# The entry of a two-layer trunk's first layer: half of the input from ScalarE's queue, five buffers for scale and shift, and another order of sums and products

## The chip, the cores and the metric

One core of a Trainium2 chip runs the whole network as one program. The metric is the device time of one launch in microseconds (us). The median of three runs of the kernel before is 2196.83 us (2194.26 to 2197.61); one further execution, recorded by the hardware profiler, took 2200.38 us. All durations below come from that execution's trace.

## What is computed

Only the very start of the network is touched: the entry of layer 0, up to its first projection.

```python
c_act = jax.nn.silu(c)                                   # c: 1 x 1024
mod = c_act @ ada_w[0] + ada_b[0]                        # 1024 x 6144 weights
sh_m, sc_m, g_m, sh_f, sc_f, g_f = jnp.split(mod, 6, axis=-1)
h = rmsnorm(x, norm_g[0, 0]) * (1 + sc_m) + sh_m         # x: 1024 positions x 1024
bcx = h @ conv_in_w[0]                                   # 1024 x 3072
b_gate, c_gate, xh = jnp.split(bcx, 3, axis=-1)          # then a 3-tap causal conv, gates, conv_out_w
```

After it come layer 0's conv output and its squared-ReLU MLP, a shared key/value side, layer 1's latent attention, and layer 1's MLP. All tensors are 32-bit floats.

## The kernel before, in words

**Tiling.** D = 1024 is cut into KD = 8 blocks k of 128 features, the positions into NT = 8 tiles t of 128 rows (`xt[0..7]`, 128x1024, named y in the profile) and into two halves of 512 positions. TensorE multiplies 32-bit values as two parts: `split_w` (L162 to L164) makes a high part on ScalarE and a low part on VectorE, and `mm` (L158 to L160) does three matmuls of 128x512 for each product. `products(w, k, half, acc)` is one feature block times one half, into three PSUM banks (the groups b, c and x of 128 output columns): nine matmuls. The phase is passed twice, for the output columns m = 0 and m = 1; the first pass also makes the operands: 16 groups of nine for m = 0, then 16 for m = 1. The remaining columns are done in another way (`all_pairs`).

**What one block k needs in the first pass.** `ada(k)` loads the scale and shift columns of `ada_w[0]` for block k, 1 MB, into the tile `aw` (three buffers) by four transfers. `ada_end(k)` (L816 to L827) sums them over eight row blocks on VectorE into `av`, each times a column of silu(c): one TENSOR_SCALAR (L820) and seven SCALAR_TENSOR_TENSOR (L822); then TensorE adds over the partitions with two matmuls by a column of ones (L824, written as four fp32 passes in the trace), and VectorE makes scale and shift, `sh` (L825, L827). `turn(k, half)` transposes four x tiles on TensorE (L832); `scaled` (L835 to L839) applies `sh` twice on ScalarE, to the high part and to the full value, and VectorE subtracts for the low part. `weights(k, m)` loads 192 KB of `conv_in_w` and splits them. `norm_x(half)` (L895 to L897) makes each x row's root of the sum of squares on ScalarE (L245, L247) and divides on VectorE.

**Order.** TensorE's and SyncE's instructions stay in the order in which the code is written (`pinned`); VectorE's and ScalarE's are set by the tile scheduler. Each engine runs its list strictly in order. SyncE issues all loads of the phase; each takes one of eight completion semaphores in turn, so a load waits until the one eight places earlier has landed, whichever engine issued it. The first half runs LAG = 2 blocks ahead: `first_half(k+1)`, then `products(k, 0)`, then `second_half(k-1)` and `products(k-2, 1)`. The small vectors (gains, biases, taps: eight transfers into the tile `raw`) are issued from ScalarE's queue (L136 to L139), x from SyncE's (`load_x`).

## Time and profile before

| | |
|---|---|
| median of three runs | 2196.83 us (2194.26 to 2197.61) |
| profiled execution | 2200.38 us, of which the recorded span is 2198.6 us |
| first product matmul (128x512) begins | 26.15 us after the span's start |
| last product of the first pass (m = 0) ends, the first of m = 1 begins | 87.08 us |
| m = 1 | 87.08 to 119.06 us |
| TensorE busy, whole span | 2105.9 us (96%) |

From 121.9 us on TensorE works almost without a pause; the first 87 us are where it stands still. In the rows of the profile a name ending in q (SPq, ACTq) is the engine's queue of issued transfers, PEld is TensorE's weight load, PEclk the granted share of TensorE's full clock, "x6" the number of instructions merged into a row, and the part in brackets is how long the engine stood idle just before, and what ended that.

### The profile page before, as it was taken

The page shows a single profiled execution, that of the slowest core. Times are in us where ns is not written, and L with a number is a line of the kernel's source. Part 1 is how long each engine was busy: PE and PEld are TensorE (multiplying, and loading weights), DVE is VectorE, ACT ScalarE, POOL GpSimd, SP SyncE. Part 2 cuts the span into 40 slices and gives each one's busy share as a digit, 9 for nine tenths or more (in the row PEclk, how much of TensorE's full clock was granted, in tenths as well). Part 3 has the DMA queues.
Part 4 walks back from the last instruction along what each step waited for, and adds up shares of the span by engine and source line. Part 5 has one row for each costly group of instructions (what it writes and reads, how often), then busy time and mean ns, then how long its engine had stood idle before and what let it go on. Part 6 is the DMA issues. An engine that isn't in the chain of part 4 may idle for free.

```text
span 2198.6 us, 25300 instructions
## 1 busy us (share of the span) xinstructions
PE 2105.9 (96%) x9702; PEld 1730.7 (79%) x9702; DVE 1523.0 (69%) x2001; ACT 1053.3 (48%) x1501; POOL 4.0 (0%) x8
## 2 busy tenths in 40 slices
PE   4999999899999999999899999999899999999998
PEld 3778878678888788888777788878688887888886
DVE  6767766866665579766788776665865665566665
ACT  4533354745454444343665555564744444444422
POOL 0000000000000000000000000000000000000000
PEclk9999999999999999999999999999999999999999
DMA  7444464246543986454214231043244553852343
GB/s 222 127 126 143 126 209 145 77 153 191 168 158 114 327 277 209 157 171 146 82 52 128 76 103 53 25 153 130 77 154 159 184 174 139 304 180 96 121 138 115
DMA packets 233551, 323.61 MB, mean 147 GB/s; under 512 B 18165, under 2 KB 141394, under 8 KB 233430
## 3 DMA queue, kind: packets, MB, share of 16 engines
q1 hardware_dynamic: 198424, 244.11, 35.5%
q10 hardware_dynamic: 35006, 77.89, 9.3%
q8 instruction: 76, 1.25, 0.2%
q14 instruction: 45, 0.37, 0.1%
HBM read 244.35 MB, written 77.59 MB: 146 GB/s over the span
## 4 chain that ended last, share of the span: by engine, by line
PE 75%; DVE 13%; ACT 6%; DMA 4%; issue 2%; ACTq 0%; SPq 0%; DVEq 0%
PE one L160 38%; PE mm L160 18%; PE big L160 9%; PE tp L160 6%; DMA raw<-in_ada_w_dram 3%; ACT junk L245 2%; PE big L1281 2%; DVE y L302 2%; DVE raw L303 2%; DVE acc L185 1%; PE tp L1307 1%; DVE y L296 1%; DVE small L1284 1%; ACT small L247 1%; PE tp L398 1%
## 5 line engine op out<-in xcount | busy, mean ns | idle before, releaser
L160 PE MATMUL one<-slot,uphi 128*128 128x512 f32 x1224 | 378.9, 391 | 0.0
L160 PE MATMUL big<-slot 128*128 128x512 f32 x1536 | 353.5, 390 | 0.9 <-DVE slot L164 0.4
L160 PEld LDWEIGHTS big<-slot 128*128 128x128 f32 x1536 | 287.6, 188 | 61.0 <-ACT y L745 1.1
L160 PEld LDWEIGHTS one<-slot,uphi 128*128 128x128 f32 x1224 | 231.3, 189 | 48.5 <-issue 0.5
L160 PE MATMUL one<-slot,uplo 128*128 128x512 f32 x612 | 241.3, 394 | 8.1 <-ACT y L564 2.3
L164 DVE TENSOR_TENSOR uplo<-raw,uphi 128x1024 fp32r<-128x1024 f32 x127 | 153.0, 1220 | 138.0 <-ACT uphi L163 137.9
L160 PE MATMUL one<-ring,ring 128*128 128x512 f32 x864 | 199.9, 392 | 5.5 <-DVE ring L164 5.5
L163 ACT ACTIVATE ring<-w 128x1024 fp32r<-128x1024 f32 x84 | 88.9, 1059 | 229.5 <-PE tp L160 121.0
L160 PEld LDWEIGHTS one<-ring,ring 128*128 128x128 f32 x864 | 162.8, 189 | 41.6 <-DVE ring L164 4.7
L163 ACT ACTIVATE uphi<-raw 128x1024 fp32r<-128x1024 f32 x127 | 134.5, 1060 | 121.1 <-PE one L160 89.4
L160 PE MATMUL mm<-slot,uphi 128*128 128x512 f32 x520 | 165.9, 400 | 9.5 <-DVE slot L363 9.3
L164 DVE TENSOR_TENSOR ring<-w,ring 128x1024 fp32r<-128x1024 f32 x84 | 102.6, 1221 | 82.5 <-ACT ring L163 82.4
L185 DVE SCALAR_TENSOR_TENSOR acc<-raw,csil,acc 128x1024 f32<-128x1024 f32 x88 | 112.7, 1281 | 44.8 <-DMA raw<-in_ada_w_dram 42.1
L160 PEld LDWEIGHTS one<-slot,uplo 128*128 128x128 f32 x612 | 115.6, 189 | 35.6 <-ACT y L489 3.3
L160 PE MATMUL mm<-ring,ring 128*128 128x512 f32 x576 | 139.6, 391 | 0.0
L160 PE MATMUL tp<-ring,ring 128*128 128x512 f32 x576 | 138.7, 389 | 0.0
L160 PEld LDWEIGHTS mm<-ring,ring 128*128 128x128 f32 x576 | 107.6, 188 | 23.5 <-issue 0.7
L160 PEld LDWEIGHTS tp<-ring,ring 128*128 128x128 f32 x576 | 108.1, 188 | 22.5
L160 PEld LDWEIGHTS mm<-slot,uphi 128*128 128x128 f32 x520 | 98.8, 192 | 32.6 <-DVE slot L363 10.8
L489 ACT ACTIVATE y<-one 128x512 f32<-128x512 f32 x66 | 39.0, 590 | 164.0 <-PE one L160 115.5
L160 PE MATMUL one<-slot,s 128*128 128x512 f32 x468 | 112.5, 389 | 0.6 <-DVE s L164 0.6
L160 PE MATMUL mm<-slot,uplo 128*128 128x512 f32 x260 | 106.3, 409 | 4.3 <-ACT slot L360 2.3
(255 smaller groups left out, 3513.0 us busy)
## 6 DMA issues: line engine op xcount, KB each, us to landing
ha<-y ACTq DMA_DIRECT2D x168, 256.0 KB, 4.3
raw<-ha SPq DMA_DIRECT2D x84, 512.0 KB, 4.1
raw<-in_ada_w_dram SPq DMA_DIRECT2D x80, 512.0 KB, 3.9
raw<-in_mlp_up_w_dram SPq DMA_DIRECT2D x70, 512.0 KB, 4.5
w<-in_mlp_down_w_dram SPq DMA_DIRECT2D x48, 512.0 KB, 6.0
raw<-hd SPq DMA_DIRECT2D x32, 512.0 KB, 4.3
hd<-y ACTq DMA_DIRECT2D x24, 512.0 KB, 2.9
xs<-raw ACTq DMA_DIRECT2D x24, 512.0 KB, 3.1
```

The costliest lines, as they stand in the source:

```text
L160: nc.tensor.matmul(out_, lhs[a], rhs[b], start=first and i == 0, stop=last and i == 2, skip_group_check=more)
L163: nc.scalar.activation(hi, src, AF.Copy)
L164: nc.vector.tensor_tensor(lo, src, hi.bitcast(F32), op=ALU.subtract)
L185: nc.vector.scalar_tensor_tensor(acc, raw, s, acc, op0=ALU.mult, op1=ALU.add)
L245: nc.scalar.activation(junk, src, AF.Square, accum_out=ss)
L247: nc.scalar.activation(rt, ss, AF.Sqrt, bias=eps_d)
L296: nc.vector.tensor_tensor(y, y, p_, op=ALU.add)
L302: nc.vector.scalar_tensor_tensor(y, y, rroot(ss), self.gmb, op0=ALU.mult, op1=ALU.mult)
L303: nc.vector.tensor_tensor(xr, xr, y, op=ALU.add)
L398: nc.tensor.transpose(p_[:, t * P:(t + 1) * P], ys[half * 4 + t][:, k * P:(k + 1) * P], ident)
L489: nc.scalar.activation(dst, x_, AF.Copy)
L1281: nc.tensor.matmul(o_, a, m_, start=j == 0, stop=j == 4 and b * HALF + w < n)
```

## The change

- **c and silu(c).** c is loaded as 8 rows of 128 and transposed by TensorE, instead of by a transfer of single values. After the exponential ScalarE runs one square root on a dummy value.
- **x.** Tiles 0 and 1 are issued from ScalarE's queue right behind the constants, 2 and 3 from the same queue after the dummy square root; 4 to 7 stay with SyncE, now ahead of the third block of scale and shift. The eight small vectors move to SyncE's queue, behind the first block.
- **Scale and shift.** Five `aw` buffers instead of three, and for k > 0 two transfers of 512 KB instead of four of 256 KB. The last of the eight row blocks is no longer summed on VectorE: TensorE multiplies it by silu(c)'s column directly. So six SCALAR_TENSOR_TENSOR per block instead of seven, and two more small matmuls.
- **Order.** LAG is gone. Half 1 of block k is made just before `products(k, 0)`, half 0 of block k+1 and `ada_end(k+1)` between `products(k, 0)` and `products(k, 1)`; the sums of block k+2 are written in two pieces around them.

The core of the diff:

```diff
-    craw = cp.tile([P, KD], F32, name="craw")
-    ld(craw, c.rearrange("o (k p) -> p (o k)", p=P))
-    nc.scalar.activation(csil, craw, AF.Exp, scale=-1.0)
-    nc.scalar.dma_start(cs, consts[:, :C_T])
+    c8 = cp.tile([KD, P], F32, name="c8")
+    ld(c8, c.rearrange("o (k p) -> (o k) p", p=P))
+    xt = [row_tile() for _ in range(NT)]
+    with pinned([mybir.EngineType.Activation]):
+        nc.scalar.dma_start(cs, consts[:, :C_T])
+        for t in range(2):
+            nc.scalar.dma_start(xt[t], x[0][t * P:(t + 1) * P, :])
...
+    craw = tp_ps()[:, :KD]
+    nc.tensor.transpose(craw, c8, ident[:KD, :KD])
+    with pinned([mybir.EngineType.Activation]):
+        nc.scalar.activation(csil, craw, AF.Exp, scale=-1.0)
+        nc.scalar.activation(small(), eps_d, AF.Sqrt)
+        for t in range(2, 4):
+            nc.scalar.dma_start(xt[t], x[0][t * P:(t + 1) * P, :])
...
-            raw = st.tile([P, KD, 2 * P], F32, tag="aw", name=nm("aw"), bufs=3)
-            for i in (0, 4):
+            raw = st.tile([P, KD, 2 * P], F32, tag="aw", name=nm("aw"), bufs=5)
+            n = KD if k else 4
+            for i in range(0, KD, n):
...
+        def ada_sum(k, i0=0, i1=KD - 1):
+            if i0 == 0:
+                accs[k] = st.tile([P, 2 * P], F32, tag="av", name=nm("av"), bufs=3)
+            acc = accs[k]
+            for i in range(i0, i1):
+                row, s = raws[k][:, i, :], csil[:, i:i + 1]
+                if i == 0:
+                    nc.vector.tensor_scalar(acc, row, s, None, op0=ALU.mult)
+                else:
+                    nc.vector.scalar_tensor_tensor(acc, row, s, acc, op0=ALU.mult, op1=ALU.add)
...
-                nc.tensor.matmul(p_[:, j:j + 1], acc[:, j * P:(j + 1) * P], ones[:, 0:1], start=True, stop=True)
+                sl = slice(j * P, (j + 1) * P)
+                nc.tensor.matmul(p_[:, j:j + 1], raws[k][:, KD - 1, sl], csil[:, KD - 1:], start=True, stop=False)
+                nc.tensor.matmul(p_[:, j:j + 1], accs[k][:, sl], ones[:, 0:1], start=False, stop=True)
...
-            w = [weights(0, 0)]
-            first_half(0)
+            ada(0)
+            load_rows()
+            raw_w = weight_rows(0, 0)
+            ada(1)
+            for t in range(4, NT):
+                ld(xt[t], x0[t * P:(t + 1) * P, :])
+            ada(2)
+            ada_sum(0)
+            norm_x(0)
+            rows()
+            w = [weights_split(raw_w)]
+            half0(0)
+            ada_sum(1)
             acc = banks6()
-            for k in range(KD + LAG):
-                if k < KD - 1:
-                    w.append(weights(k + 1, 0))
-                    first_half(k + 1)
-                if k < KD:
-                    products(w[k], k, 0, acc)
-                if k == LAG:
-                    norm_x(1)
-                    second_half(0)
-                if k >= LAG:
-                    if k - LAG < KD - 1:
-                        second_half(k - LAG + 1)
-                    products(w[k - LAG], k - LAG, 1, acc)
+            w.append(weights(1, 0))
+            ada(3)
+            products(w[0], 0, 0, acc)
+            half0(1)
+            norm_x(1)
+            half1(0)
+            products(w[1], 1, 0, acc)
+            ada_sum(2)
+            half1(1)
+            products(w[0], 0, 1, acc)
+            w.append(weights(2, 0))
+            half0(2, lambda: ada_sum(3, 0, 4))
+            products(w[1], 1, 1, acc)
+            for k in range(2, KD):
+                if k < KD - 2:
+                    ada(k + 2)
+                if k == 2:
+                    ada_sum(3, 4)
+                half1(k)
+                products(w[k], k, 0, acc)
                 if k < KD - 1:
+                    half0(k + 1, lambda: ada_sum(k + 2, 0, 4) if k < KD - 2 else None)
+                w.append(weights(k + 1, 0) if k < KD - 1 else weights(0, 1))
+                if k < KD - 2:
+                    ada_sum(k + 2, 4)
+                products(w[k], k, 1, acc)
```

Three places of the instruction lists show what moves. The first is SyncE's list of loads at the very start (SPq in the profile; "waits" names the completion semaphore that must have counted, DMAHW0 to DMAHW7). Before, with craw for c, w for the weights, aw for scale and shift, y for x:

```order
L115 DMA craw<-in_c_dram 128x8x1
L115 DMA w_201<-in_conv_in_w_dram 128x3x128
L115 DMA aw_207<-in_ada_w_dram 128x4x128 x2
L115 DMA aw_207<-in_ada_w_dram 128x4x128 [waits DMAHW1_49]
L115 DMA aw_207<-in_ada_w_dram 128x4x128 [waits DMAHW2_49]
L115 DMA y_175<-in_x_dram 128x1024 [waits DMAHW4_49]
L115 DMA y_176<-in_x_dram 128x1024 [waits DMAHW0_49]
L115 DMA y_177<-in_x_dram 128x1024 [waits DMAHW1_49]
L115 DMA y_178<-in_x_dram 128x1024 [waits DMAHW2_49]
L115 DMA w_276<-in_conv_in_w_dram 128x3x128 [waits DMAHW3_49]
L115 DMA aw_282<-in_ada_w_dram 128x4x128 [waits DMAHW4_49]
```

And in the changed kernel (raw is the tile of the small vectors; the tiles of x that are not here, y_80 to y_83, are on ScalarE's list):

```order
L114 DMA raw_91<-in_norm_g_dram 64x128 [waits DMAHW0_49]
L114 DMA raw_91<-in_conv_w_dram 24x128 [waits DMAHW1_49]
L114 DMA raw_91<-in_conv_b_dram 8x128 [waits DMAHW2_49]
L114 DMA raw_91<-in_kv_norm_g_dram 8x128 [waits DMAHW3_49]
L114 DMA raw_91<-in_q_a_norm_g_dram 3x128 [waits DMAHW4_49]
L114 DMA raw_91<-in_kv_a_norm_g_dram 2x128 [waits DMAHW5_49]
L114 DMA raw_91<-in_ada_b_dram 96x128 [waits DMAHW7_49]
L114 DMA raw_91<-in_kv_ada_b_dram 16x128 [waits DMAHW0_49]
L114 DMA w_206<-in_conv_in_w_dram 128x3x128 [waits DMAHW1_49]
L114 DMA aw_208<-in_ada_w_dram 128x8x128 [waits DMAHW3_49]
L114 DMA aw_208<-in_ada_w_dram 128x8x128 [waits DMAHW4_49]
L114 DMA y_84<-in_x_dram 128x1024 [waits DMAHW5_49]
```

The weights of block 0 and everything behind them now stand behind eight small loads, each of which waits for one of the first eight loads or for another small one. The four x tiles that stood ahead of block 1's scale and shift are gone from this list, and the other four now begin behind it.

The second place is TensorE's list up to the first product, before: the transposes of half 0 of block 1 (tp<-cs,y), the sum over partitions of its scale and shift (tp<-ones,av), and the nine products of block 0, half 0 (slot):

```order
L832 MATMUL tp_287<-cs,y_175 128x128 [waits DVE_49]
L832 MATMUL tp_287<-cs,y_176 128x128
L832 MATMUL tp_287<-cs,y_177 128x128
L832 MATMUL tp_287<-cs,y_178 128x128
L824 MATMUL tp_292<-ones,av_293 128x1 [waits DVE_49,PE_49,Activation_49]
L824 MATMUL tp_292<-ones,av_293 128x1
L160 MATMUL mm_275<-slot_161,w_204 128x512
L160 MATMUL mm_275<-slot_161,w_203 128x512 x2
L160 MATMUL mm_274<-slot_161,w_204 128x512
L160 MATMUL mm_274<-slot_161,w_203 128x512 x2
L160 MATMUL one_273<-slot_161,w_204 128x512
L160 MATMUL one_273<-slot_161,w_203 128x512 x2
```

In the changed kernel the products of block 0, half 0 come first, and these twelve rows stand between them and the products of block 1, half 0 (y_80 to y_83 are half 0 of x, y_84 to y_87 half 1):

```order
L845 MATMUL tp_317<-csil,aw_208 128x1 [waits DMAHW3_49]
L846 MATMUL tp_317<-ones,av_285 128x1
L845 MATMUL tp_317<-csil,aw_208 128x1 [waits DMAHW4_49]
L846 MATMUL tp_317<-ones,av_285 128x1
L854 MATMUL tp_324<-cs,y_80 128x128 [waits PE_49,Activation_49]
L854 MATMUL tp_324<-cs,y_81 128x128
L854 MATMUL tp_324<-cs,y_82 128x128
L854 MATMUL tp_324<-cs,y_83 128x128
L854 MATMUL tp_365<-cs,y_84 128x128 [waits DVE_49]
L854 MATMUL tp_365<-cs,y_85 128x128
L854 MATMUL tp_365<-cs,y_86 128x128 [waits DVE_49]
L854 MATMUL tp_365<-cs,y_87 128x128 [waits DVE_49]
```

The first product has less ahead of it, the second group more: it now stands behind transposes of half 1, which before came after the third group.

The third place is VectorE's list where half 1 of x is normalised. Before (small and y_179 to y_182 belong to that; sh_195 is the scale and shift of block 2, av the sums, slot a low part):

```order
L839 TENSOR_TENSOR slot_161<-q_169,slot_161 128x512 [waits Activation_49]
L822 SCALAR_TENSOR_TENSOR av_339<-aw_324,csil,av_339 128x256 [waits DVE_49]
L252 RECIPROCAL small_411<-small_409 128x1 [waits Activation_49]
L822 SCALAR_TENSOR_TENSOR av_339<-aw_324,csil,av_339 128x256 [waits DVE_49]
L897 TENSOR_SCALAR y_179<-y_179,small_411 128x1024 [waits DMAHW5_49,DVE_49]
L825 SCALAR_TENSOR_TENSOR sh_195<-tp_338,g_189,b_190 128x1 [waits PE_49]
L827 TENSOR_TENSOR sh_195<-tp_338,bias 128x1
L252 RECIPROCAL small_419<-small_417 128x1 [waits Activation_49]
L897 TENSOR_SCALAR y_180<-y_180,small_419 128x1024 [waits DMAHW6_49,DVE_49]
L839 TENSOR_TENSOR slot_161<-q_170,slot_161 128x512 [waits Activation_49]
L164 TENSOR_TENSOR w_367<-w_364,w_366 128x384 [waits DMAHW1_49,Activation_49]
L252 RECIPROCAL small_427<-small_425 128x1 [waits Activation_49]
```

In the changed kernel (sh_186 is the scale and shift of block 1, y_86 and y_87 the last two tiles of half 1):

```order
L847 SCALAR_TENSOR_TENSOR sh_186<-tp_317,g_183,b_184 128x1 [waits PE_49]
L849 TENSOR_TENSOR sh_186<-tp_317,bias 128x1
L263 RECIPROCAL small_353<-small_351 128x1 [waits Activation_49]
L927 TENSOR_SCALAR y_86<-y_86,small_353 128x1024 [waits DMAHW7_49,DVE_49]
L837 TENSOR_SCALAR av_382<-aw_215,csil 128x256 [waits DMAHW2_49,DMAHW1_49]
L839 SCALAR_TENSOR_TENSOR av_382<-aw_215,csil,av_382 128x256 [waits DVE_49]
L168 TENSOR_TENSOR w_302<-w_299,w_301 128x384 [waits DMAHW3_49,Activation_49]
L839 SCALAR_TENSOR_TENSOR av_382<-aw_215,csil,av_382 128x256 [waits DVE_49] x2
L863 TENSOR_TENSOR slot_169<-q_177,slot_169 128x512 [waits Activation_49]
L263 RECIPROCAL small_361<-small_359 128x1 [waits Activation_49]
L839 SCALAR_TENSOR_TENSOR av_382<-aw_215,csil,av_382 128x256 [waits DVE_49]
L927 TENSOR_SCALAR y_87<-y_87,small_361 128x1024 [waits DMAHW0_49,DVE_49]
```

Normalising the third tile now stands behind block 1's scale and shift, which waits for TensorE, and normalising the fourth behind sums, a split of weights and a low part besides. From about the 190th row of TensorE's list, the 160th of VectorE's, the 100th of ScalarE's and the 50th of SyncE's on, the two kernels list the same operations in the same order.

More of the change, by code (lines that the diff above doesn't have):

```diff
@@ L37 @@
 ROWS = 8
-LAG = 2
 PAIRS = (D_FF // P - ROWS) // 2
@@ L164, in split_w @@
         nc.vector.tensor_tensor(lo, src, hi.bitcast(F32), op=ALU.subtract)
-    nc.vector.tensor_scalar(csil, csil, 1.0, None, op0=ALU.add)
-    nc.vector.reciprocal(csil, csil)
-    nc.vector.tensor_tensor(csil, csil, craw, op=ALU.mult)
     def ada_acc(accp, w, col, bias_row=None):
@@ L233, in ada_bc @@
         return [begin] + [lambda k=k: st["t"][k]() for k in range(KD)] + [end]
+    craw = tp_ps()[:, :KD]
[5 more added lines that the diff above has]
+            nc.scalar.dma_start(xt[t], x[0][t * P:(t + 1) * P, :])
+    nc.vector.tensor_scalar(csil, csil, 1.0, None, op0=ALU.add)
+    nc.vector.reciprocal(csil, csil)
+    nc.vector.tensor_tensor(csil, csil, craw, op=ALU.mult)
     bg = []
@@ L790, in conv_phase @@
         st = pool("st", "right")
-        xt = [row_tile() for _ in range(NT)]
-        def load_x(half):
-            for t in range(4 * half, 4 * half + 4):
-                ld(xt[t], x0[t * P:(t + 1) * P, :])
-        p_ = tp_ps()
-        nc.tensor.transpose(p_[:, :VEC_ROWS], vrows[:VEC_ROWS, :], ident[:VEC_ROWS, :VEC_ROWS])
-        nc.vector.tensor_copy(vecs, p_[:, :VEC_ROWS])
-        p_ = tp_ps()
-        nc.tensor.transpose(p_[:, :BIAS_ROWS], brows[:BIAS_ROWS, :], ident[:BIAS_ROWS, :BIAS_ROWS])
@@ L833, in turn, with scaled @@
             return p_
-        def scaled(k, p_, dst, name):
+        def scaled(k, p_, dst, name, between=None):
             hi, lo = ops[name][k % 4]
@@ L853, in weights @@
             return w
+        def weights(k, m):
+            return weights_split(weight_rows(k, m))
         late = []
```

73 lines of the change are left out of this document (37 added, 36 removed).

## The prediction

> **What bounds the kernel now.** I read the busy times by stretch first. Columns: each engine's busy time, PEclk, the share of the 16 DMA engines' time, GB/s.
>
> ```profile
> 0.00:26.00 26.00, 5.19 (x18) 3.39 (x18) 14.69 (x44) 11.02 (x20) 0.20 (x4) 1.00 0.97 284
> 26.00:40.90 14.90, 8.09 (x32) 6.43 (x31) 12.14 (x32) 8.53 (x17) 0.00 (x0) 0.89 1.06 297
> 40.90:51.20 10.30, 9.44 (x32) 7.35 (x32) 8.30 (x19) 4.23 (x6) 0.00 (x0) 0.66 0.06 17
> 51.20:70.80 19.60, 17.80 (x99) 14.37 (x97) 13.38 (x32) 10.45 (x16) 0.00 (x0) 1.00 0.50 138
> 70.80:87.00 16.20, 15.81 (x69) 12.69 (x69) 9.75 (x18) 11.05 (x18) 0.00 (x0) 0.89 0.14 40
> 87.00:119.00 32.00, 32.00 (x143) 26.50 (x142) 21.07 (x34) 11.79 (x22) 0.95 (x1) 1.00 0.48 139
> ```
>
> TensorE has no idle time from 87 us on; what can be won lies before. The first 41 us have the DMA engines full (0.97, 1.06), then they stand nearly still (0.06). Next, whom TensorE waited for in 0 to 87 us, and whom SyncE's queue waited for in 0 to 90 us (total us, times, longest):
>
> ```profile
> PE tp L824 <- DVE av L822: 10.6, 4, 6.9
> PE tp L832 <- DVE y L897: 5.9, 4, 2.1
> PE tp L800 <- DMA raw<-in_kv_ada_b_dram: 2.5, 1, 2.5
> ```
>
> ```profile
> SPq L115 <- DVE sh L827: 19.7, 3, 14.4
> ```
>
> TensorE waits for sums and for normalised x; the loads wait for a free aw buffer, which comes when a block's sums are done. Third, the chain that ended last (start, duration), which prices the pieces:
>
> ```profile
> 0.74 3.26 DMA craw<-in_c_dram
> ...
> 41.95 2.77 PE mm L160 x6
> 44.72 1.28 PE one L160 x3
> ...
> 51.25 0.44 PE tp L832 x4
> 51.69 0.35 PE tp L824 x4
> ...
> 54.69 4.08 DMA aw<-in_ada_w_dram
> ...
> 60.63 4.05 DMA aw<-in_ada_w_dram
> ...
> 87.08 1.36 PE mm L160 x6
> 88.44 2.72 PE one L160 x12
> ```
>
> Nine product matmuls cost 2.04 us at full clock (half of 1.36 + 2.72) and 4.05 us at half (2.77 + 1.28). Four transposes cost 0.44, a block's scale and shift 0.35 for two matmuls, and twice the chain stands 4 us on a load of aw. Last, the first product and the beginnings of the groups k, half 0:
>
> ```profile
> 26.15 2.91 PE L160 MATMUL mm<-slot,w 128*128 128x512 f32 x6
> ...
> 40.96 0.98 PE L824 MATMUL tp<-ones,av 128*128 128x1 f32 x4 [6.88 <-DVE av L822]
> ...
> 51.89 1.63 PE L160 MATMUL mm<-slot,w 128*128 128x512 f32 x6
> ...
> 57.35 1.63 PE L160 MATMUL mm<-slot,w 128*128 128x512 f32 x6
> ...
> 63.61 1.65 PE L160 MATMUL mm<-slot,w 128*128 128x512 f32 x6
> ...
> 70.42 0.58 PE L824 MATMUL tp<-ones,av 128*128 128x1 f32 x4 [1.39 <-DVE av L822]
> 70.86 2.04 PE L160 MATMUL mm<-slot,w 128*128 128x512 f32 x6
> ...
> 77.13 1.52 PE L160 MATMUL mm<-slot,w 128*128 128x512 f32 x6
> ```
>
> By 51.25 five of the sixteen groups of the first pass are done; the other eleven take until 87.08. A block's period is 5.46, 6.26, 7.25 and 6.27 us; only the first is free of a late load and of half clock. After 87.08 both kernels list the same work in the same order, so I take what is won or lost at that mark to stay to the end.
>
> **The change, step by step.** Everything is a time at which something begins or ends in the span.
>
> *The entry.* Rows of before:
>
> ```profile
> 7.14 0.32 ACTq L139 DMA_DIRECT2D raw<-in_kv_ada_b_dram  x1
> 10.46 0.48 DVE L822 SCALAR_TENSOR_TENSOR av<-aw,csil,av 128x256 f32<-128x256 f32 x1 [1.31 <-DMA aw<-in_ada_w_dram]
> 13.10 0.42 PE L800 MATMUL tp<-cs,raw 112*128 112x112 f32 x1 [2.49 <-DMA raw<-in_kv_ada_b_dram]
> 14.21 0.30 ACT L247 ACTIVATE small<-small,eps_d 128x1 f32<-128x1 f32 x1
> 18.58 0.29 ACT L247 ACTIVATE small<-small,eps_d 128x1 f32<-128x1 f32 x1
> 20.00 0.75 DVE L897 TENSOR_SCALAR y<-y,small 128x1024 f32<-128x1024 f32 x1
> ```
>
> The first eight loads now are constants, c, block 0 and x0, x1: 2.3 MB, 8 us at 284 GB/s, so landed by about 10, as block 0 was before (10.46). The last small load, kv_ada_b, is issued then, because SyncE's list has to wait there for the first eight. Landing took 6.0 us before (7.14 to 13.10, beside a full queue) and 3.3 us for c. I take 3.3, since nothing large is left ahead of it in its own queue: 13.3, at worst 16. Behind it follow TensorE's transpose (0.42), the copy and two small operations (0.6), scale and shift of block 0, now four matmuls instead of two, so twice 0.98 at the slow rate of 40.96 (15.7), `sh` (0.4) and the low part of w (0.5, by L839 below, for 384 columns instead of 512): 16.6. ScalarE's square roots come every 1.46 us before (14.21 to 18.58 for three). In the changed kernel the first stands behind the split of w, which is issued right behind kv_ada_b and so lands about 13.5; four end by 18.8, so VectorE, not ScalarE, sets the pace from 16.6.
>
> ```profile
> L822 DVE SCALAR_TENSOR_TENSOR av<-aw,csil,av 128x256 f32<-128x256 f32 x41 | 19.5, 481 | 0.8
> L838 ACT ACTIVATE slot<-tp,sh 128x512 fp32r<-128x512 f32 x11 | 8.5, 777 | 21.4 <-DVE sh L827 17.7 <-PE tp L832 2.7 <-DVE small L252 1.0
> L839 DVE TENSOR_TENSOR slot<-q,slot 128x512 fp32r<-128x512 f32 x7 | 4.8, 688 | 3.9 <-ACT q L838 3.9
> ```
>
> Its list for the four tiles holds four divisions (0.75), each with a reciprocal of one column (my estimate 0.2), and six sums of 128x256 (0.48): 6.7 us if nothing overlaps. Neighbours on different tiles overlap a little, so I take 5.7: done at 22.3. One transpose (0.5) and one ScalarE pass (0.78) make the **first product begin at 23.6** instead of 26.15. Its second matmul waits for the low part (behind a fifth division, 25.0); eight matmuls at half clock end at 28.9.
>
> *The second group* pays for that. The block's scale and shift (four matmuls, 1.9) end at 30.8, `sh` at 31.2. VectorE's list then holds a division, a TENSOR_SCALAR, four sums, a split, a low part and the last division: 4.9 us by the same rows and overlap, so y_87 is done at 36.1 and **products (1, 0) begin at 36.5**. TensorE has stood still from 31 to 36, and the clock rows show what such a wait does:
>
> ```profile
> 38.00:39.00 1.00, 0.00 (x0) 0.00 (x0) 0.93 (x3) 0.00 (x0) 0.00 (x0) 0.50 1.01 283
> ...
> 47.00:48.00 1.00, 0.98 (x5) 0.58 (x3) 0.93 (x3) 1.00 (x2) 0.00 (x0) 0.50 0.00 0
> 48.00:49.00 1.00, 0.33 (x1) 0.00 (x1) 0.72 (x3) 1.00 (x3) 0.00 (x0) 1.00 0.00 0
> ...
> 72.00:73.00 1.00, 1.00 (x4) 0.82 (x3) 0.11 (x1) 0.86 (x2) 0.00 (x0) 0.50 0.67 191
> ```
>
> PEclk is 0.50 in the wait and until 48, 7 us after the work resumed at 40.96. With 7 us again: (1, 0) ends at 40.6, four transposes at 41.5, (0, 1) at 44.5 (2 us slow, the rest fast), scale and shift (0.7) and transposes at 45.7, (1, 1) at 47.7. (2, 0) waits for its low part until 48.4 and ends at 50.4: five groups, 0.9 us ahead of before. The Trainium skill ("TensorE: Matmul & The Clock Gate", the states table in Part 1) has the full clock return after about 3.4 us of sustained work; by that the slow stretch would cost 1.8 us less and the sum below would be 2188.9. The trace speaks against it at this place, with 7 us.
>
> Block 2's scale and shift and block 1's weights are due on VectorE's list at about 32 and 33; all bytes up to them are 8.2 MB, 29 us at 284 GB/s, so they land at about 31. That cover is thin: each us beyond it moves the mark by as much.
>
> *The other eleven groups.* Per block TensorE needs 4.08 + 0.88 + 0.70 = 5.66 us, VectorE 7 x 0.48 + 0.5 + 2 x 0.69 + 0.4 = 5.6 without overlap, ScalarE 4 x 0.78 + 0.5 = 3.6. One sum less saves VectorE 0.48; two small matmuls more cost TensorE 0.35. From below the period is 5.46 (the clean one), from above 7.25. I take 5.7, nearest to the clean one, because the loads are covered: a block is 1.25 MB, 4.4 us at 284 GB/s, and with five buffers it is issued two blocks ahead. Were that cover gone, 4 us a block would come back (54.69, 60.63). Five periods from 48.4 give 76.9, two groups 4.1: **81.0 instead of 87.08, a gain of 6.1 us**, 0.9 of it from the entry and 5.2 from the waits for aw.
>
> The remaining edits (c as rows, the early square root that takes a table load out of the first x tile's way) lie ahead of the landing of the biases, which hides them. The profiled execution took 2200.38, so the same kind of run should give 2194.3; it lies 3.55 above the median of three, 2196.83, which becomes **2190.7 us**.
>
> **The rivals.**
>
> *The second group isn't slow* (chance 0.15). If VectorE reaches y_87 sooner, TensorE stays at full clock: (1, 0) costs 2.0 less, (0, 1) 1.0 and transposes 0.5, so 77.5; with the biases at 12 and a period of 5.46, 75: gains of 9.6 to 12, 2187 to 2185. For it: the clock fell before only about 4 us after TensorE stopped. Against: five listed VectorE operations stand there.
>
> *The entry gives nothing, or the period stays* (0.30). The DMA engines were full to 41 us whatever queue a load came from, and the changed list puts eight small loads and their waits ahead of w. With the biases at 16 the entry is lost again, 83.7, a gain of 3.4; with the mean period of before, 6.31, and the entry as I have it, 84.1, a gain of 3.0; with both, nothing is left: 2194 to 2197. The Trainium skill ("DMA: Bandwidth & Descriptors", Issuing engines are not separate DMA queues) says that loads begun by several engines run on the same 16 DMA engines and save only the time of issuing; by it, x from ScalarE's queue brings nothing. The row of the first 26 us (0.97) agrees that there was no free engine to be had.
>
> *Slower* (0.10): the clock. Row 72 to 73 us shows PEclk at 0.50 after an idle time of 1.4 us only. If short waits for low parts recur in each block, the clock can stay down: a matmul costs 0.45 instead of 0.227. 99 of them are left after 50.4; from 27 slow ones on (6.1 / 0.223) the change is slower than before, at 60 by 7 us, 2204. Against it: between 51 and 69 us the same kind of waits left PEclk at 1.00.
>
> *My forecast*: 0.45.
>
> **How the numbers follow.** About 0.2% (4.4 us) is what a measurement of this kernel can tell from no change. Faster by more than that: the forecast case and the first rival, 0.60. Within: the second rival, 0.30. Slower: 0.10. For 8 in 10 the range leaves out the best part of the first rival and nearly all of the last: 2184 to 2198.
>
> **What would show it.** In the profile after: first product at 23.6; TensorE idle for 4 to 5 us before the second group, released by the divisions of half 1, PEclk 0.50 behind it; no wait for aw on the chain after 50 us and half-0 groups 5.7 us apart; m = 1 begun at 81.0 and 32.0 us long. I am wrong if the biases land much later than 13.3, if the load of block 2 or of w is late at 34, or if the lead at 81 is eaten up further on.

## The result and the profile after

The changed kernel takes **2207.31 us** (median of five, 2204.03 to 2208.43), beside 2197.61 for the kernel before in the same runs: ratio 1.0038 [1.0023, 1.0053]. By the ratio it is slower by some 8 us, where 6 us less had been forecast. The profiled execution took 2208.18 us, with a span of 2206.4, 7.8 above the span of before.

The first pass did get shorter. Rows of the changed kernel's timeline (start, duration, engine, line; in brackets the idle time before it and what ended it):

```profile
16.30 0.52 ACT L167 ACTIVATE w<-w 128x384 fp32r<-128x384 f32 x1 [4.25 <-DMA w<-in_conv_in_w_dram]
...
19.95 0.35 DVE L837 TENSOR_SCALAR av<-aw,csil 128x256 f32<-128x256 f32 x1 [1.68 <-DMA aw<-in_ada_w_dram]
...
26.05 0.80 PE L164 MATMUL mm<-slot,w 128*128 128x512 f32 x1 [0.87 <-ACT slot L860]
...
37.85 0.47 PE L854 MATMUL tp<-cs,y 128*128 128x128 f32 x1 [3.41 <-DVE y L927]
```

The first product begins at 26.05, as before. ScalarE stood 4.25 us for block 0's weights ahead of the first root, and VectorE 1.68 us for block 1's aw ahead of a division. The second group waits for the last division of x's second half. The chain of waits, from there to m = 1:

```profile
38.32 2.56 PE mm L164 x6
40.88 1.28 PE one L164 x3
42.16 0.85 PE tp L854 x4
43.02 2.47 PE one L164 x9
...
49.30 1.39 PE mm L164 x6
50.69 0.69 PE one L164 x3
51.50 0.22 PE tp L846 x2
51.72 0.22 PE tp L845 x2
51.95 0.22 PE tp L846 x2
52.17 0.50 PE tp L854 x4
...
78.78 1.39 PE mm L164 x6
...
83.21 1.39 PE mm L164 x6
84.59 2.78 PE one L164 x12
```

From 42 us TensorE never waits in this pass, and no load of aw stands on the chain: the waits that the change was to take away are gone. From 49.30 to 78.78 five periods take 29.48, 5.9 each. m = 1 begins at 83.21, 3.9 us ahead of before. But look at the last two rows: twelve products take 2.78 us where the same chain of before has 2.72. m = 1 ends at 115.95, so it is 32.7 us long in place of 32.0, with TensorE busy throughout. This goes on: the same stretch far from the change, in the windows of the changed kernel and then of before (in brackets the number of matmuls):

```profile
500.00:1000.00 500.00, 495.27 (x2182) 405.06 (x2181) 340.58 (x375) 220.44 (x254) 0.00 (x0) 1.00 0.59 196
```

```profile
500.00:1000.00 500.00, 494.93 (x2198) 408.01 (x2197) 345.34 (x378) 221.36 (x255) 0.00 (x0) 1.00 0.60 199
```

TensorE is as busy, at the same PEclk, and gets through 16 matmuls fewer. And it isn't all matmuls. Groups by line and shape (busy us, mean ns), changed kernel, then before:

```profile
L164 PE MATMUL one<-slot,uphi 128*128 128x512 f32 x1224 | 382.9, 394 | 0.0
...
L164 PE MATMUL mm<-ring,ring 128*128 128x512 f32 x576 | 139.5, 390 | 0.0
```

```profile
L160 PE MATMUL one<-slot,uphi 128*128 128x512 f32 x1224 | 378.9, 391 | 0.0
...
L160 PE MATMUL mm<-ring,ring 128*128 128x512 f32 x576 | 139.6, 391 | 0.0
```

Products of slot by uphi got slower, those of ring by ring did not. From m = 1's beginning to the span's end the changed kernel needs 2123.2 us, before 2111.5: **11.7 us more for the same list of work**.

What differs there is where the operands lie. The tile c8, 512 bytes per partition, took the place of craw, 32 bytes, in the first pool `cp` (which holds an 8-float tile named "even" at its foot, L116). All pools stacked on the left behind it moved by 480 bytes: y from 45792 to 46272, the first slot of arB from 78560 to 79040, w from 127712 to 128192. The pools stacked on the right (uphi, ring, arA, cA) stayed. I set the start-to-start distances of neighbouring 128x512 fp32r products in each trace beside the operands' addresses in the program. Each product counts by its own two operands, and those are left out behind which the stationary remainder changes. In the kernel before, all operands of these products were 32 past a multiple of 64:

| moving and stationary address, modulo 64 | before: count, mean ns | after: count, mean ns |
|---|---|---|
| 32 and 32 | 7799, 227.3 | 4921, 227.8 |
| 0 and 0 | none | 851, 228.7 |
| 0 and 32 | none | 1733, 233.3 |
| 32 and 0 | none | 168, 235.2 |

1901 products with unequal remainders, 6 to 8 ns each, are 11.7 us. The equal ones were slower than before's as well, by 0.5 and 1.4 ns, which by the same table is 3.7 us more, so the agreement to a tenth is luck. That was the theory to test: **the addresses of the tiles behind c8, not the order of the work, made the kernel slower.** The rivals: the new order leaves something behind that slows the later stages, or it is the trace's chance.

### The profile page after: what moved, and what is told of

The parts are those of the page before. It is cut to its first block, busy times and chain, and to the rows that moved or that the text cites. A ratio compares the mean times of both kernels' runs of the same rounds, so it can differ in the third digit from the quotient of the medians.

```text
span 2206.4 us, 25334 instructions
## 1 busy us (share of the span) xinstructions
PE 2122.4 (96%) x9735; PEld 1732.5 (79%) x9735; DVE 1519.9 (69%) x1993; ACT 1054.1 (48%) x1502; POOL 4.0 (0%) x8
## 4 chain that ended last, share of the span: by engine, by line
PE 77%; DVE 12%; ACT 6%; DMA 3%; issue 2%; SPq 0%; ACTq 0%; DVEq 0%
PE one L164 38%; PE mm L164 18%; PE big L164 9%; PE tp L164 6%; DMA raw<-in_ada_w_dram 2%; PE big L1328 2%; ACT junk L256 2%; DVE y L313 2%; DVE raw L314 2%; PE tp L1354 1%; DVE acc L184 1%; DVE y L307 1%; DVE small L1331 1%; ACT small L258 1%; ACT z L1185 1%
```

## The experiments

**The stacks moved by 32 and by 64 bytes.** Nothing else changes; each engine's list of instructions stays the same. Changed kernel, and the same edit in the kernel before; after_plus64 takes 24 floats:

```diff
-    cp.tile([P, 8], F32, name="even")
+    cp.tile([P, 16], F32, name="even")
```

> The changed kernel with one tile of the first pool 32 bytes longer, so that every tile of the left-hand pools begins at 32 instead of 0 in units of 64 bytes, as in the kernel before; every instruction list is unchanged. Address theory: matmuls of 512 columns whose two operands differ by 32 in that remainder start 233 to 235 ns apart in the changed kernel's trace (about 2000 of them), those whose operands agree 227 to 228; all will agree, some 12 us are won: 2195, that is 0.999 of the kernel before. Rival, the changed order or loads cost time later in the program: still 2207, 1.004.

> The kernel before with the same 32 bytes more, nothing else; its left-hand tiles then begin at 0 instead of 32. Address theory: it becomes slower by about 12 us, 2209 or 1.0055, with pairs of operands that differ at 233 to 235 ns start to start and nothing changed in the first 26 us. Rival, order or loads: no difference, 1.000 within 0.001.

> The changed kernel with the same tile 64 bytes longer: all addresses of the left-hand pools move, but their remainder by 64 stays as in the changed kernel. Address theory: no gain, 2207, 1.004. If any move of the addresses helps (another granularity than 64 bytes, or chance): about 2195.

| run | median us | ratio to before | unequal remainders |
|---|---|---|---|
| after_plus32 | 2194.83 | 0.9987 [0.9979, 0.9996] | none |
| before_plus32 | 2209.3 | 1.0058 [1.0047, 1.0070] | 1903 at 233 to 234 ns |
| after_plus64 | 2203.7 | 1.0043 [1.0029, 1.0057] | as after |

32 bytes take the loss out of the changed kernel and put it into the kernel before; 64 bytes do nothing. A further execution of after_plus32 gives its profile:

> The changed kernel with the left-hand pools put back by 32 bytes, looked at once more for its profile, whose first one fell on a disturbed execution. If the addresses are all that it changes: first product at 26, second group at 38, half 0's groups 5.9 us apart as in the changed kernel, m=1 at 83.2 but 32.0 us long in place of 32.7, and the 128x512 fp32r products 227 ns apart everywhere; span 2194 to 2196. Rival: something in the first pass is also moved by the shift, and m=1 begins elsewhere than at 83.

Its time was 2192.4. Chain of waits of after_plus32_again, then of before_plus32, at m = 1:

```profile
81.04 1.37 PE mm L164 x6
82.42 2.72 PE one L164 x12
```

```profile
84.44 1.36 PE mm L160 x6
85.80 2.78 PE one L160 x12
```

The price per twelve products goes with the address, 2.72 or 2.78, whichever kernel it is. m = 1 began at 81.04, not at 83.2, and before_plus32 began it at 84.44, not at before's 87.08: single executions differ by 2 to 3 us in the first pass. The clock has a part in it: a pair of small matmuls at 31 us took 0.22 here and 0.43 in the changed kernel's trace, and after the wait ahead of the second group the full clock was back at 40.67 here and at 43.72 there (the clock's records in the stored traces).

**The right-hand stack moved instead.** The left one stays where c8 put it.

```diff
     cp = pool("cp")
+    pad = pool("pad", "right")
+    pad.tile([P, 8], F32, name="pad")
```

> The changed kernel, word for word, with one 32-byte tile added at the foot of the right-hand stack of pools: the left-hand pools stay 0 past a multiple of 64 and the right-hand ones come there too, where they had been 32 past it. If what costs is that a product's two operands have different remainders by 64, the cost goes as it did when the left-hand pools were moved back: 128x512 fp32r products start 227 ns apart again and the time is about 2195 (ratio to before 0.9985 to 0.9995). Rival: the left-hand pools lie badly at a remainder of 0, whatever the other operand's: every product is then 233 ns, and the time is 2220 or more; or only total room and order count, and it stays at 2207.

Measured: 2192.96, ratio 0.9986 [0.9977, 0.9995]; all 7808 pairs at 227.3 ns with both operands at 0. So no place is bad by itself: what counts is how the two operands lie to each other. The rival that the new order of the work costs later falls too, since in all of these runs every engine's list was that of the kernel that was edited.

**Products by themselves.** Five kernels that leave the whole network out and run lots of 128x512 fp32r products, so that only addresses differ. The last three take the products in the network's order (m the moving tile, s the stationary one, j the offset):

```python
for n, (a, b) in enumerate(((1, 0), (0, 1), (0, 0))):
    sl = P * (a * 3 + g + 6 * (k % 2))
    ml = HALF * (b + 2 * (k % 2))
    yield (banks[3 * (t % 2) + g], s[:, 8 * j + sl:8 * j + sl + P], m[:, ml:ml + HALF],
           k == 0 and n == 0, k == 7 and n == 2)
```

> Leaves the whole network out: 256 matmuls of 128x512 to warm up, then nine lots of 128 with the moving operand's row beginning at 0, 32 or 64 bytes (by 128) and the stationary one's at 0, 32 or 64, each lot on a line of its own; the output is one product copied eight times. Address theory: 227 us per thousand in the five lots that agree by 64 (0/0, 0/64, 32/32, 64/0, 64/64), so about 29.1 us each, and 233 to 235, so 29.9 us, in the four others. If what counts is an absolute remainder of one operand: whole rows of the table slow. If addresses do not matter: all nine 29.1.

> Leaves the whole network out: twelve lots of 128x512 fp32r products, made nearer to the network's than the first such kernel. In lots 2 to 6 (256 products each, after a first warm lot) the stationary operand goes through eight 512 B slices, the moving one through four 2 KB slices, sixteen products are summed in a PSUM bank and four banks are taken in turn; moving and stationary begin 0 and 0, 0 and 32, 32 and 0, 32 and 32, 0 and 64 bytes past a multiple of 64. Lots 7 to 9 (128 products) keep one slice of each, lots 10 to 12 (256) close the sum after each product; offsets 0 and 0, 0 and 32, 32 and 32. If the remainders by 64 of the two operands alone make the pitch: 58.1 us (227 ns each) for the lots with equal remainders and 59.7 (233 ns) for 0 and 32 and 32 and 0; by half for the lots of 128. If the difference needs what else runs in the network (the other engines' reads and writes beside the products): all lots of a kind within 0.3 us of each other. If the first kernel's missing difference came from its single slices or its closed sums, it shows in lots 2 to 6 and not in 7 to 9 or not in 10 to 12.

> Leaves the whole network out: eight lots of 288 128x512 fp32r products in the order of the first layer (three sums side by side, each block three products: low part by high, high by low, high by high), with moving and stationary operand at 96 and 96 (twice, the first a warm lot), 64 and 96, 96 and 64, 64 and 64, 0 and 96, 0 and 0, 32 and 32 bytes past a multiple of 128. If the remainders by 64 make the pitch once the order is the network's: 65.3 us (227 ns) for lots 2, 5, 7 and 8, and 67.2 (233 ns) for lots 3, 4 and 6. Rival: as in the two kernels before, products alone do not show it, and all lots lie within 0.8 us.

All three missed: in operand_pairs nine lots of 128 took 29.30 to 29.98 us, in operand_pairs_near lots 2 to 6 took 59.49, 59.73, 59.96, 59.49 and 58.61, and in operand_pairs_kernel_like all lots behind the warm one lay between 66.92 and 67.47 (232 to 234 ns), the equal remainders by 64 too. Neither single slices, closed sums nor the order of the network made the difference. So a remainder by 64 is not the rule. Next, a stationary tile farther off, and other engines at work:

> Leaves the whole network out: seven lots of 288 128x512 fp32r products in the network's order, moving and stationary operand at 96 and 96 (lots 1, 2, 4, 6) or 64 and 96 (lots 3, 5, 7) bytes past a multiple of 128; the stationary operand lies 8 KB behind the moving one in lots 1 to 3 and 113 KB behind it in lots 4 to 7; beside lots 6 and 7 VectorE and ScalarE go through 128x1024 tiles without a stop. If the distance of the operands is what kept the products by themselves from showing the network's difference: lot 4 takes 65.3 us (227 ns) and lot 5 67.2 (233 ns), as lots 6 and 7. If the other engines' traffic is: lots 2 to 5 all near 67, and 65.3 to 66 against 67.2 or more only in lots 6 and 7. If neither: all lots within 0.5 us of 67, and the rule stays open.

Chain of waits; L85 and L87 are the near lots at 96 and 96, and 64 and 96; L89 and L91 the far ones:

```profile
75.91 66.92 PE pp L85 x288
142.84 67.20 PE pp L87 x288
210.04 65.28 PE pp L89 x288
275.32 67.22 PE pp L91 x288
```

The far lot reached the network's pace without any other engine at work; beside a busy VectorE and ScalarE the same two far lots began their products 226.8 and 233.3 ns apart, so that traffic changed nothing. But the far tiles of the fast lot also began an exact multiple of 256 bytes apart (112896), the near ones 128 off that (8320). The last kernel separates the two:

> Leaves the whole network out: after a warm lot twelve lots of 288 128x512 fp32r products in the network's order, the moving operand at one place. Lots 2 to 9: the stationary operand 8 KB behind it, its start differing from the moving one's by 0, 32, 64, 96, 128, 160, 192 and 224 bytes modulo 256; lots 10 to 13: 113 KB behind it, by 0, 32, 128 and 192. In operand_pairs_far the lot that reached 227 ns was farther off and also the only one whose two starts were equal modulo 256. If the difference modulo 256 decides: 65.3 us (227 ns) in lots 2 and 10, 66.9 to 67.5 (232 to 234 ns) in 3 to 7 and 9, 11 and 12, 65.9 (229 ns) in 8 and 13. If the distance does: lots 2 to 9 all 66.9 or more, save 65.9 at 192, and lot 12 at 65.3 like lot 10.

Its chain; L81 to L95 are near, differing by 0, 32, 64 and so on up to 224 modulo 256, L97 to L103 far, by 0, 32, 128 and 192:

```profile
76.51 65.33 PE pp L81 x288
141.84 67.19 PE pp L83 x288
209.03 67.20 PE pp L85 x288
276.23 67.47 PE pp L87 x288
343.70 66.93 PE pp L89 x288
410.63 67.19 PE pp L91 x288
477.82 65.92 PE pp L93 x288
543.74 67.19 PE pp L95 x288
610.93 65.29 PE pp L97 x288
676.22 67.19 PE pp L99 x288
743.41 66.93 PE pp L101 x288
810.34 67.19 PE pp L103 x288
```

**Equal starts modulo 256: 226.8 ns; every other difference tried, in steps of 32 bytes: 229 to 234**, near or far. (Only 192 is 65.92 near and 67.19 far, a miss of the forecast. By 512 these two differ by 192 and by 448; whether that decides was not tried.) With it the three misses fall into place: their tiles began 128 apart, so no lot had equal starts. In the network the operands of each product with equal remainders by 64 lie whole multiples of 256 from each other, and those with unequal ones 32 off that, so a remainder by 64 told the same there as one by 256.

The mechanism isn't shown. The Trainium skill ("SBUF — State Buffer", A bandwidth-pool intuition that's wrong) gives TensorE a second, independent port for loading weights; if that load is what meets the moving operand's reads, 227 against 233 ns says that they are not independent. The traces narrow down which pair of operands it is. In the changed kernel 129 products have equal starts themselves, but the next product's stationary operand lies unequal to their moving one: the next start comes after 232.4 ns, where the same places of after_plus32_again have 227.1. In another 166 only the next product's own two operands are unequal to each other: 228.6 against 228.1. So the pair that costs is the moving operand of one product and the stationary operand of the next, as it would be if the next load met the running reads. Only five places would tell whether a product's own pair costs too, which is too few, and no run changes the load by itself.

**Five buffers alone, in the kernel before.**

```diff
-            raw = st.tile([P, KD, 2 * P], F32, tag="aw", name=nm("aw"), bufs=3)
+            raw = st.tile([P, KD, 2 * P], F32, tag="aw", name=nm("aw"), bufs=5)
```

> The kernel before with five buffers for scale and shift's weights in place of three and nothing else; all pools keep their remainder by 64. If what is won in the first pass stays to the end once the addresses stay: the waits for aw in half 0's groups go, m=1 begins 2 to 5 us sooner than 87.08, and the time is 2193 to 2195 (ratio 0.998 to 0.999). Rival: the transfers themselves set the pace, and more buffers only queue them earlier: m=1 begins at 87 and the ratio is 1.000.

Measured: 2195.44, ratio 0.9999 [0.9989, 1.0008]. Chain of waits:

```profile
53.35 4.31 DMA aw<-in_ada_w_dram
...
59.49 3.80 DMA aw<-in_ada_w_dram
...
84.15 1.37 PE mm L160 x6
```

The two waits for aw stay, so buffers alone don't take them away. Which of the other edits does, the order of loads and sums or the larger transfers, with the buffers or without, was not separated. m = 1 begins 2.9 us sooner than in the profile of before, but the buffers didn't do that: before_plus32, with three buffers and every list as in before, begins it at 84.44. The profile of before is the late one of the three; PEclk from 70.8 to 87.0 us is 0.89 in it (a row of the prediction) and 1.00 in before_plus32. So the forecast's mark came true by luck, and the time is the rival's.

**The eighth term back on VectorE**, on top of the 32 bytes, so that a block has two small matmuls, not four.

```diff
-        def ada_sum(k, i0=0, i1=KD - 1):
+        def ada_sum(k, i0=0, i1=KD):
...
-                nc.tensor.matmul(p_[:, j:j + 1], raws[k][:, KD - 1, sl], csil[:, KD - 1:], start=True, stop=False)
-                nc.tensor.matmul(p_[:, j:j + 1], accs[k][:, sl], ones[:, 0:1], start=False, stop=True)
+                nc.tensor.matmul(p_[:, j:j + 1], accs[k][:, sl], ones[:, 0:1], start=True, stop=True)
```

> The changed kernel with its pools put back by 32 bytes (as in the run before, 2194.8) and the eighth term of each block's sum on VectorE again, so that TensorE has 2 in place of 4 small products per block. TensorE-bound groups: half 0's groups come 5.5 us apart in place of 5.9, six of them, m=1 begins at about 80.7, the time is 2192 (ratio 0.9975). Rival: VectorE's 0.48 us more per block makes it late in each group, the groups stay 5.9 apart or more, and the time is 2195 or above.

Measured: **2190.24, ratio 0.9975 [0.9965, 0.9986]**, the lowest ratio here, though its interval touches those of after_right32 and entry_pinned; faster than both kernels. Chain:

```profile
60.84 0.34 PE tp L845 x4
...
66.27 0.34 PE tp L845 x4
...
79.45 1.36 PE mm L164 x6
```

0.34 in place of 0.78 per block and 5.43 per period. VectorE had the room, as the theory of TensorE-bound groups had it, and m = 1 came 1.3 us sooner still than it said.

**The entry.** Three orders, all with the 32 bytes. In entry_pinned all four engines are held to the written order in the entry, block 0's weights are loaded ahead of the small vectors, and block 1's ahead of the third block of scale and shift:

```diff
-        with pinned([mybir.EngineType.PE, mybir.EngineType.SP]):
+        with pinned(everything):
             ada(0)
+            raw_w = weight_rows(0, 0)
             load_rows()
-            raw_w = weight_rows(0, 0)
...
+            raw_w1 = weight_rows(1, 0)
             ada(2)
...
-            w.append(weights(1, 0))
+            w.append(weights_split(raw_w1))
```

> The changed kernel put back by 32 bytes, with all four engines held to the written order in the entry, block 0's weights ahead of the small rows and block 1's weights ahead of scale and shift's block 2. If the entry was late because ScalarE waited for w ahead of the first divisor and VectorE for block 1's aw ahead of a division: first product at 19 to 22 us in place of 26.05, second group at 29 to 34 in place of 37.98, m=1 at 77 to 80 in place of 83.2, and the time 2190 to 2192 (ratio 0.997). Rival: transfers set the entry's pace: second group at 37 to 38, m=1 at 83, time 2195.

Measured: 2192.96, ratio 0.9988 [0.9980, 0.9996], so no more than the 32 bytes alone. The first product began at 22.0, at the late end of what was expected; the second group and m = 1 missed it. The chain has

```profile
29.66 1.04 ACT junk L256 x2
...
36.64 2.56 PE mm L164 x6
...
81.83 1.36 PE mm L164 x6
```

ScalarE starts the squares of x's second half only at 29.66, and the second group is at 36.64. The next kernel puts them ahead, with the eighth term on VectorE, and the groups in the order (0,0), (0,1), (1,0), (1,1) (cut from the diff against the changed kernel):

```diff
             products(w[0], 0, 0, acc)
+            norm_x(1)
+            w.append(weights_split(raw_w1))
+            half1(0)
+            products(w[0], 0, 1, acc)
             half0(1)
-            norm_x(1)
-            half1(0)
             products(w[1], 1, 0, acc)
+            half1(1)
+        with pinned([mybir.EngineType.PE, mybir.EngineType.SP]):
             ada_sum(2)
-            half1(1)
-            products(w[0], 0, 1, acc)
```

> The changed kernel with its pools put back by 32 bytes, eight terms on VectorE as in the run before (2190.2 by itself), block 0's weights ahead of the small rows, all four engines held to the written order up to 30 us, and the first products in the order (0,0), (0,1), (1,0), (1,1), with x's second half normalised ahead of block 1's half 0. In entry_pinned the second group stood at 36.64 for x's second half, whose squares ScalarE began at 29.55 though the tiles had come by about 25. If that order is what is late: second group at 30 to 31.5, m=1 at 74 to 76, and the time 2184 to 2187 (ratio 0.995 to 0.996). Rival: the transfers of the second half and of scale and shift's blocks 2 and 3 then come late instead: a wait for aw or w opens between 34 and 50 us, m=1 begins at 78 or later, and the time is 2189 or above.

Measured: 2200.13, ratio 1.0023 [1.0013, 1.0033], m = 1 at 88.32: the rival's side of the forecast. VectorE's timeline:

```profile
29.25 0.35 DVE L837 TENSOR_SCALAR av<-aw,csil 128x256 f32<-128x256 f32 x1 [2.05 <-DMA aw<-in_ada_w_dram]
...
32.86 0.35 DVE L837 TENSOR_SCALAR av<-aw,csil 128x256 f32<-128x256 f32 x1 [0.55 <-DMA aw<-in_ada_w_dram]
```

The scheduler had put the sums of blocks 2 and 3 ahead of divisions, and VectorE stood in front of them. The last one holds VectorE and ScalarE to the written order up to block 4's sum (cut from the diff against entry_reordered):

```diff
-        with pinned([mybir.EngineType.PE, mybir.EngineType.SP]):
             ada_sum(2)
             w.append(weights(2, 0))
-            half0(2, lambda: ada_sum(3, 0, 4))
+            half0(2)
             products(w[1], 1, 1, acc)
...
+            ada_sum(4)
+        with pinned([mybir.EngineType.PE, mybir.EngineType.SP]):
```

> As entry_reordered, with VectorE and ScalarE held to the written order up to and with block 4's sum, so that no sum for a later block can stand in VectorE's list ahead of a division or subtraction that TensorE waits for. In entry_reordered VectorE stood at 29.25 and 32.86 for aw of blocks 2 and 3 ahead of the divisions of x's second half, and m=1 began at 88.2. If that list is what made the entry late: second group at 30 to 32, m=1 at 75 to 78, and the time 2185 to 2188 (ratio 0.995 to 0.9965). Rival: the transfers themselves are late: TensorE then waits as long for the sums of blocks 2 and 3, second group by 32 but m=1 at 80 or later, and the time is 2190 or above.

Measured: 2210.02, ratio 1.0066 [1.0052, 1.0080]: the rival's numbers, but not its mechanism. The second group began at 31.9, and from 20 to 100 us no wait of VectorE's ended with a transfer, so the transfers do not set it. VectorE's timeline and TensorE's waits in the first 125 us show the price:

```profile
46.25 0.69 DVE L862 TENSOR_TENSOR b<-raw,b 128x512 fp32r<-128x512 f32 x1 [5.51 <-ACT raw L859]
```

```profile
PE tp L845 <- DVE av L839: 12.4, 3, 6.3
```

VectorE now stands idle 5.51 us in front of a subtraction while block 2's sum, whose data had landed by 29.25 in entry_reordered, is written behind it; TensorE waits 12.4 us for sums, and m = 1 begins at 98.38. Both orders lose by what stands ahead in VectorE's list, one by sums ahead of divisions, one by subtractions ahead of sums. An order that gives both up was not found.

**Whether the mark stays to the end.** From m = 1's first row on the chain to the span's end, all runs that have a profile of the whole network:

| kernels | us from m = 1 to the end |
|---|---|
| equal starts: before, before_five_buffers | 2111.5, 2111.3 |
| equal starts: after_plus32_again, after_right32, plus32_sum8, entry_pinned, entry_reordered, entry_held | 2109.6, 2107.0, 2109.7, 2105.8, 2108.4, 2110.5 |
| unequal: after, before_plus32, after_plus64 | 2123.2, 2123.6, 2118.6 |

## Why the prediction was wrong, point by point

- **The step that failed**: "After 87.08 both kernels list the same work in the same order, so I take what is won or lost at that mark to stay to the end." The list is the same, its addresses are not. With equal starts the rest takes 2105.8 to 2111.5 us in eight profiles, whatever the mark; with unequal ones 2118.6 to 2123.6. The step cost 11.7 us in the profiled pair: 2198.6 - 3.9 + 11.7 = 2206.4. The edit that did it was among those I costed at nothing ("c as rows"): I priced its instructions and not its tile. The diff shows it: craw has 8 floats per partition, c8 128, in the first pool of the stack.
- **The mark**: 83.21, not 81.0. (2, 0) begins at 49.30 instead of 48.4, 0.9; five periods take 29.48 instead of 28.5, 1.0; the last two groups 4.43 instead of 4.1, 0.3. That after_plus32_again has 81.04 is luck: its (2, 0) began at 47.30, its five periods took 29.31, its last two groups 4.43.
- **First product at 23.6: wrong**, 26.05. The small vectors were in time, the weights were not: I let w land at about 13.5, and it came at 16.30, 5.5 us after its issue at 10.81. ScalarE's roots, not VectorE, were then late, and VectorE's wait for block 1's aw came on top. entry_pinned, with w earlier and that wait behind the divisions, begins at 22.0, which shows this for the two together.
- **The second group at 36.5: late by 1.5** (37.98), for the reason given, VectorE's list.
- **The slow clock behind the wait: right in kind, 5.9 us instead of 7.** The nine products from 38.32 take 3.84 us, and the full pace is back within the group at 43.02. Yet PEclk (the third number from the right) reads 1.00 there, in the first row below. The second is of after_plus32_again, where the products up to 40.67 ran at the same half pace:

```profile
38.00:43.00 5.00, 5.00 (x15) 4.02 (x16) 4.96 (x14) 1.86 (x3) 0.00 (x0) 1.00 1.08 293
```

```profile
38.00:43.00 5.00, 5.00 (x20) 4.01 (x19) 4.88 (x13) 2.74 (x5) 0.00 (x0) 0.73 1.09 278
```

  The stored trace of the changed kernel has no record of the clock ahead of 43.72 us, where one of full clock begins, and the view prints 1.00 where there is no record. So that 1.00 is no measurement. By the records the full clock was back 5.9 us after TensorE resumed at 37.85, and 3.8 us (after_plus32_again) and 7.0 us (before) after it resumed there. The Trainium skill ("TensorE: Matmul & The Clock Gate", the states table in Part 1) has about 3.4 us, as the time of at least one busy window; all three are longer.
- **No aw wait on the chain after 50: right.** The period of 5.7 became 5.9: the four small matmuls cost 0.78 with their gap instead of 0.70, transposes 0.94 instead of 0.88, products 4.17 instead of 4.08. Little of this is the addresses: with equal starts, in after_plus32_again, the products of a period take 4.15 and the period 5.87.
- **m = 1 32.0 us long: wrong**, 32.7. It was the first trace of what the prediction had named as a sign of being wrong, a lead that is eaten up further on.
- **The rivals.** Slower came true, but not by the half clock in short waits, which did not recur: TensorE waited for nothing from 42 us to m = 1. Of the second rival the first half came true, by another cause: the entry gave nothing at the first product, for w and the waits above and not for the biases, which were there by 13.5.
- **The gain of 6.1** was too large even with the addresses put right: the change then measures 0.9986 and 0.9987, 3 us faster, within 0.2% of no change. The mark of before is a good part of that. I took 87.08, and the 3.55 us by which that execution lay above the median I carried over unchanged; before_plus32, with the same lists, has its mark at 84.44, and before_five_buffers at 84.15. Against these the changed order in its four profiles (after, after_plus64, after_right32 and after_plus32_again, 81.04 to 83.21) is 1 to 3 us early. So the waits for aw went as forecast, and the size was read off one late execution.

## What to carry to other kernels

A tile added to or resized in the first pool moves every pool stacked behind it: price a change's tiles as well as its instructions, by the addresses of the two operands of the bulk of the matmuls. Here they had to start equal modulo 256 bytes, which a 32-byte tile in either stack brought back. Take the mark that a gain is counted from out of more than one execution. When TensorE is busy throughout and yet gets through fewer matmuls, compare the distance of their starts by pairs of operands before looking for a wait. And an engine's list in strict order loses by whatever stands ahead: that a sum is early is no gain if it waits in front of a division.

## What the runs showed that I had not expected

- A 128x512 fp32r product begins 226.8 ns after the last where moving and stationary operand start equal modulo 256 bytes, and 229 to 234 ns after it elsewhere: 65.33 against 65.92 to 67.47 us for 288. In this network that is 12 us of 2200, from one 512-byte tile.
- The pair is one product's moving operand and the next one's stationary operand: 232.4 against 227.1 ns in 129 places where only these two lie unequal.
- The other engines' traffic is not needed for it, nor does distance matter where the starts are equal (65.33 at 8 KB, 65.29 at 113 KB).
- PEclk prints 1.00 for a stretch from which the trace has no record of the clock: nine products took 3.84 us there instead of 2.04.
